# Centring the RWKV-7 values before the scan, and evicting each gram by one masked product

## The chip, the cores and the metric

The kernel runs on one NeuronCore of a Trainium2 chip. The metric is the device time of one execution in microseconds (us); what is compared is the median of the runs. A difference of 0.3% is about 9 us here.

The core has a matrix engine (PE, with its weight loads shown apart as PEld), a vector engine (DVE), an activation engine (ACT), a general engine (POOL) and a queue that issues most transfers (SP). Each engine works through its own instructions in the order in which they were put there.

## The reference

A decoder trunk of two layers over 1024 tokens of width 1024. Layer 0 mixes tokens with an RG-LRU, layer 1 with RWKV-7; each layer then has cross-attention into 256 memory tokens and a squared-ReLU MLP, and every part is wrapped in RMS norms. The change touches only the RWKV-7 mixer. Per head (16 heads of 64), a 64x64 state runs over the tokens, and the 64 outputs of a token are normalised to mean zero and unit variance:

```python
def step(state, inp):
    r_t, w_t, k_t, v_t, a_t, b_t = inp
    sa = einsum('bhij,bhj->bhi', state, a_t)
    state = state * w_t + sa[..., None] * b_t + v_t[..., None] * k_t
    y_t = einsum('bhij,bhj->bhi', state, r_t)
    return state, y_t
mean = jnp.mean(y, axis=-1, keepdims=True)
var = jnp.mean(jnp.square(y - mean), axis=-1, keepdims=True)
yn = (y - mean) * lax.rsqrt(var + RWKV_GN_EPS)      # then gain gn_g, offset gn_b
bonus = jnp.sum(rh * kh * r_k, axis=-1, keepdims=True) * vh
out = (yn + bonus) * g @ w_o
```

The index i of the state comes from the value v alone, and everything that is done to the state is linear in v. So subtracting from each v its mean over i subtracts from each y its mean over i. The bonus uses v itself.

## The kernel before, in words

All matrix work is in float32, in two ways: large products as three products of split halves (`mm3`, L317 to L319), small ones as one float32 product (`mm`). The trace records such a float32 product as two MATMUL records, a transpose as one.

The mixer `rwkv` goes through K, R and V phases, each a loop over eight blocks f of 128 features, and then the scan. In the V phase `evac_v(f)` copies the finished block `vt` (features x tokens) from PSUM (L1488), turns it to tokens by eight transposes of 128x128 in two PSUM banks (L1503), copies each bank to `vk` on ACT (L1504), stores `vk` to DRAM in `Vd` and forms the bonus from the same `vt` (L1520, L1521).

The scan works through 16 chunks of 64 tokens, two chunks to a load of 128 tokens. The work of chunk c has three parts, interleaved in the text of the loop (L1699 to L1765):

- The recurrence: products W (L1723), a copy of W on ACT (L1725), products U (L1745), a scaling on DVE into `sv` (L1747), products S (L1753) and an addition on DVE into the next chunk's `sv` (L1755), which the next W needs. POOL forms the decayed state `pcs` from it (L1732). The output Y is accumulated by L1728 and L1761 and copied to `y` by ACT (L1763).
- The grams of chunk c+1 (`scan_gram`, groups 0 to 3): four products per group (L1618) into one bank; DVE multiplies the wanted parts by triangular masks into `gt` (twice L1621 on 64 partitions, once L1624); ACT copies two quarters of `mv` into the places of `gt` that no gram fills (twice L1623); PE transposes the keys that POOL scaled (`scan_scale`, L1606, then L1632), and ACT copies them into `gt` (L1633). A group's `gt` feeds W, S and Y of the next chunk.
- The norm of chunk c-1: `post_mean` sums y on DVE (L1643) and POOL turns the sum to minus the mean (L1644); `post_var` adds that on DVE (L1650), squares on ACT (L1651), sums on DVE (L1652), and POOL forms the reciprocal root (L1653, L1654); `post_norm` multiplies on DVE (L1660). `flip_out(c-2)` transposes back to features (L1667) and applies gain and bonus (L1672 on DVE, L1673 on POOL).

The order of instructions on each engine is not that of the text. A planner that knows costs and dependences places each instruction when its inputs are due, earlier text first; `behind` and `pin` bind an instruction behind those already traced on its engine. The square of L1651 is pinned: it comes behind the last ACT instruction of group 1 of the next gram.

Loads for a pair of chunks are issued one pair ahead on SP (`load`, L1561 and L1565; `load_solved`, L1576; `load_late`, L1589 and L1593). Behind the scan follows the output projection with `b_w_o`, whose weights are split on ACT and DVE (L232, L233) from chunk 13 on, while the scan still runs.

Of the kernel before, what the change touches and what calls it, by code (L numbers as in the profile page):

```python
# [7 lines left out]
F32 = mybir.dt.float32  # L8
F32R = mybir.dt.float32r
AF = mybir.ActivationFunctionType  # L10
ALU = mybir.AluOpType
AX = mybir.AxisListType
# [1084 lines left out]
def rwkv_consts(self):  # L1097
    nc = self.nc
    c = self.const
    self.omu = c([128, 48], "omu")  # L1100
    nc.vector.tensor_scalar(self.omu, self.colv("mu", 48), -1.0, 1.0, ALU.mult, ALU.add)
    self.w0h = c([128, 8], "w0h")
    nc.vector.tensor_scalar(self.w0h, self.colv("w0"), 0.5, None, ALU.mult)
    self.a0h = c([128, 8], "a0h")
    nc.vector.tensor_scalar(self.a0h, self.colv("a0"), 0.5, None, ALU.mult)
    self.kah = c([128, 8], "kah")
    nc.vector.tensor_scalar(self.kah, self.colv("k_a"), 0.5, None, ALU.mult)
    self.kam = c([128, 8], "kam")
    nc.vector.tensor_scalar(self.kam, self.colv("k_a"), -1.0, 1.0, ALU.mult, ALU.add)
    self.nkk = c([128, 8], "nkk")  # L1110
    nc.vector.tensor_scalar(self.nkk, self.colv("k_k"), -1.0, None, ALU.mult)

    self.ind = c([128, 2], "ind")
    nc.gpsimd.memset(self.ind, 0.0)
    nc.gpsimd.memset(self.ind[0:64, 0:1], 1.0)
    nc.gpsimd.memset(self.ind[64:128, 1:2], 1.0)

    self.id64 = c([128, 64], "id64")
    nc.vector.tensor_add(self.id64, self.ident[:, 0:64], self.ident[:, 64:128])

    self.mask1 = c([128, 128], "mask1")
    nc.gpsimd.memset(self.mask1, 1.0)
    self.mask2 = c([128, 64], "mask2")
    nc.gpsimd.memset(self.mask2, 1.0)
    for h in range(2):
        r = slice(h * 64, h * 64 + 64)

        nc.gpsimd.affine_select(self.mask1[r, 0:64], self.mask1[r, 0:64], pattern=[[1, 64]], base=0,
                                channel_multiplier=-1, compare_op=ALU.is_ge, fill=0.0)
        nc.gpsimd.affine_select(self.mask2[r, :], self.mask2[r, :], pattern=[[1, 64]], base=-1,  # L1130
                                channel_multiplier=-1, compare_op=ALU.is_ge, fill=0.0)
    self.db = c([128, 256], "db")
    self.pc = c([128, 128], "pc")

    self.ones = c([128, 128], "ones")
    nc.gpsimd.memset(self.ones, 0.0)
    for h in range(2):
        nc.gpsimd.memset(self.ones[h * 64:h * 64 + 64, h * 64:h * 64 + 64], 1.0)


def rwkv_make_mix(self, X, i, hf, out, js=range(KT // 2)):
# [58 lines left out]
def rwkv(self, X, xt, lw_wa, lw_g, post):  # L1200
    nc, I = self.nc, self.I
    mm = nc.tensor.matmul
# [19 lines left out]
    for hf in range(2):  # L1222
        o = hf * 512
# [12 lines left out]
        if hf:  # L1236
            h = maps[0][2]
# [4 lines left out]
    h = maps[1][2]  # L1242
# [10 lines left out]
    hr = [slice(0, 64), slice(64, 128)]  # L1253
# [231 lines left out]
    def evac_v(f, p):  # L1485
        cs = slice(f * 128, f * 128 + 128)
        vt = self.unit()
        nc.scalar.copy(vt, p)  # L1488
        if f == 1:

            self.depth, self.ahead = DA
            with self.behind():
                self.advance(self.taken - 1)
        pr, kp = ld.pop(f)
        nc.vector.scalar_tensor_tensor(pr, pr, self.col("r_k", f), kp, ALU.mult, ALU.mult)

        if f % 2 == 0:
            vk[:] = [self.unit() for _ in range(2)]
        for e in range(2):
            pt = self.bank()  # L1500
            for i in range(4):
                tt = e * 4 + i
                nc.tensor.transpose(pt[:, i * 128:i * 128 + 128], vt[:, tt * 128:tt * 128 + 128], self.ident)  # L1503
            nc.scalar.copy(vk[e].rearrange("p (t h g i) -> p t h g i", h=2, g=2, i=64)[:, :, :, f % 2, :],  # L1504
                           pt.rearrange("p (t h i) -> p t h i", h=2, i=64))
            if f % 2 and e == 0:

                for d in range(2):
                    for h in range(2):
                        nc.sync.dma_start(sv0[d][hr[1 - h], h * 512 + (f - 1) * 64:h * 512 + (f + 1) * 64],  # L1510
                                          vk[0].rearrange("p (t h i) -> p t h i", h=2, i=128)[hr[d], 0, h, :])
            if f % 2:
                for h in range(2):
                    nc.sync.dma_start(Vd[e * 512:e * 512 + 512, h, (f - 1) * 64:(f + 1) * 64].rearrange("(t p) i -> p t i", p=128),
                                      vk[e].rearrange("p (t h i) -> p t h i", h=2, i=128)[:, :, h, :])
        g1 = self.unit()
        for e in range(2):
            s = slice(e * 512, e * 512 + 512)
            bp = self.bank()
            mm(bp, self.ones, pr[:, s], start=True, stop=True)  # L1520
            nc.vector.tensor_mul(vt[:, s], vt[:, s], bp)  # L1521
            gp = self.bank()
            self.mm3(gp, (g2[0][:, cs], g2[1][:, cs]), (hg[0][:, s], hg[1][:, s]), True, True)
            nc.scalar.activation(g1[:, s], gp, AF.Copy, scale=self.col("gn_g", f))
            nc.vector.scalar_tensor_tensor(vt[:, s], vt[:, s], self.col("gn_b", f), gp, ALU.add, ALU.mult)
        for src, dst in ((g1, G1d), (vt, G2d)):
            for h in range(2):
                nc.sync.dma_start(dst[(f % 2) * 64:(f % 2) * 64 + 64, (f // 2) * 2 + h, :], src[h * 64:h * 64 + 64, :])
# [11 lines left out]
    cst, prs, z, mvb = {}, {}, [], []  # L1540
# [67 lines left out]
    def scan_gram(c, groups):  # L1608
        if c >= 16:
            return  # L1610
        s = cst[c]
        for g in groups:
            gt = self.unit()[:, 0:768].rearrange("p (q h w) -> p q h w", q=2, h=2)
            pv = self.bank(g).rearrange("p (q h w) -> p q h w", q=2, h=2)
            for pp in range(2):
                q = 2 * g + pp
                for h in range(2):
                    mm(pv[:, pp, h, :], s["st"][q // 4][:, q % 4].rearrange("p w t -> p (w t)"), s["mv"][:, q, h], start=True, stop=True)  # L1618
            for h in range(2):
                o = hr[1 - h]  # L1620
                nc.vector.tensor_tensor(gt[o, :, h, 0:64], pv[o, :, h, 0:64],  # L1621
                                        self.mask2[o].unsqueeze(1).broadcast_to([64, 2, 64]), ALU.mult)
                nc.scalar.copy(gt[hr[h], :, h, 0:64], s["mv"][hr[h], 2 * g:2 * g + 2, h, 0, :])  # L1623
            nc.vector.tensor_tensor(gt[:, :, :, 64:128], pv[:, :, :, 64:128],  # L1624
                                    self.mask1[:, 0:64].unsqueeze(1).unsqueeze(1).broadcast_to([128, 2, 2, 64]), ALU.mult)
            if c < 15:
                if g % 2 == 0:
                    s["tp"] = self.bank(g // 2).rearrange("p (q h i) -> p q h i", q=4, h=2)
                tp = s["tp"][:, 2 * (g % 2):2 * (g % 2) + 2]
                for pp in range(2):  # L1630
                    q = 2 * g + pp
                    nc.tensor.transpose(tp[:, pp].rearrange("p h i -> p (h i)"), s["sc"][:, q * 128:q * 128 + 128], self.ident)  # L1632
                nc.scalar.copy(gt[:, :, :, 128:192], tp)  # L1633
            s["gts"].append(gt)
# [2 lines left out]
    yq = lambda t: t.rearrange("p (q i) -> p q i", i=64)  # L1637
    over = lambda t: t.unsqueeze(2).broadcast_to([128, 8, 64])

    def post_mean(c):  # L1640
        s = cst[c]
        s["n"] = mean, var = [self.sp.tile([128, 8], F32, name=self.nm("g8"), tag="g8", bufs=8) for _ in range(2)]
        nc.vector.tensor_reduce(mean, yq(s["y"][:, 0:512]), op=ALU.add, axis=AX.X)  # L1643
        nc.gpsimd.tensor_scalar(mean, mean, -1.0 / 64, 0.0, ALU.mult, ALU.add)  # L1644

    def post_var(c):
        s = cst[c]
        y = s["y"]
        mean, var = s["n"]
        nc.vector.tensor_tensor(yq(y[:, 0:512]), yq(y[:, 0:512]), over(mean), ALU.add)  # L1650
        self.pin(nc.scalar.activation(y[:, 512:1024], y[:, 0:512], AF.Square))  # L1651
        nc.vector.tensor_reduce(var, yq(y[:, 512:1024]), op=ALU.add, axis=AX.X)  # L1652
        nc.gpsimd.tensor_scalar(var, var, 1.0 / 64, 64e-5, ALU.mult, ALU.add)  # L1653
        nc.gpsimd.tensor_tensor(var, var, self.nhalf[:, :8], ALU.pow)  # L1654

    def post_norm(c):
        s = cst[c]
        y = s["y"]
        mean, var = s["n"]
        POST(nc).tensor_tensor(yq(y[:, 0:512]), yq(y[:, 0:512]), over(var), ALU.mult)  # L1660

    def flip_out(c):
# [36 lines left out]
    for c in range(16):  # L1699
# [62 lines left out]
                   stop=(m == 1 and q == 3))  # L1762
        nc.scalar.copy(y[:, 0:512], yp)  # L1763
        s["y"] = y
        post_mean(c)  # L1765
    post_var(15)
    post_norm(15)
    self.depth, self.ahead = 2, 3
# [58 lines left out]
```

## Time and profile before

| what | value |
|---|---|
| median of 3 runs | 2956.07 us (2955.89, 2956.07, 2964.06) |
| the profiled execution, its own time | 2958.01 us |
| its span, first to last instruction | 2956.3 us |
| PE busy | 2846.8 us, 96% |
| DVE busy | 1807.8 us, 61% |
| ACT busy | 1365.6 us, 46% |
| POOL busy | 860.7 us, 29% |
| mean granted clock of PE | 0.988 of 2.4 GHz |

The busy shares are averages over stages that differ. The V phase lies between 1653 and 1780 us of the span, the scan between 1780 and 1984 us. A group of the trace gives a line of the code, the engine, the operation with its output and input, the shapes, the count, the busy time and the mean duration of one. The duration of a MATMUL record holds the way through the array, so records overlap; the time that a matmul costs is read from the distance between starts.

### The profile page before, as it was taken

To read this page: it belongs to the slowest core of one execution; us is meant where nothing else is said; L and a number is where in the kernel's file an instruction comes from. 1 tells how busy PE (TensorE), PEld (TensorE's weight loads), DVE (VectorE), ACT (ScalarE), POOL (GpSimd) and SP (SyncE) were. 2 spreads that over 40 slices of the span, in tenths; PEclk is the share of its full clock that TensorE was granted. 3 is DMA by queue.
4 is the path that set the end of the run, shared out by engine and by line. 5 is a ranking of instruction groups with operands and counts; after the bars stand their busy time and mean duration, and the time that the engine had idled before them with its cause. 6 is when DMAs were issued, how large, how long until landed. Compare 5 with 4: busy or idle time off the path is not lost.

```text
span 2956.3 us, 42688 instructions
## 1 busy us (share of the span) xinstructions
PE 2846.8 (96%) x16987; PEld 2373.4 (80%) x16987; DVE 1807.8 (61%) x2110; ACT 1365.6 (46%) x1981; POOL 860.7 (29%) x951
## 2 busy tenths in 40 slices
PE   7999999999999999999999998989999999999998
PEld 6888798887888888887777677878788788888886
DVE  5576552557455677877585626883345745557778
ACT  5465342446444543448552524452344544454333
POOL 2000110022666500021486215652002366650001
PEclk9999999999999999999999999999999999999999
DMA  7212362123444644432656989952312344464443
GB/s 255 78 49 74 98 207 75 48 83 98 157 149 149 239 166 152 164 114 94 182 158 191 236 217 220 205 137 93 100 43 79 100 146 157 153 224 175 157 170 115
DMA packets 383847, 421.91 MB, mean 143 GB/s; under 512 B 91440, under 2 KB 294432, under 8 KB 383648
## 3 DMA queue, kind: packets, MB, share of 16 engines
q1 hardware_dynamic: 371616, 379.19, 42.6%
q0 software_dynamic: 11568, 39.41, 3.7%
q8 instruction: 133, 2.18, 0.3%
q14 instruction: 66, 0.54, 0.1%
q10 hardware_dynamic: 464, 0.59, 0.1%
HBM read 283.79 MB, written 134.74 MB: 142 GB/s over the span
## 4 chain that ended last, share of the span: by engine, by line
PE 83%; DVE 7%; DMA 3%; issue 2%; ACT 2%; POOL 2%; SPq 1%; DVEq 0%; POOLq 0%; ACTq 0%
PE q L317 15%; PE q L319 15%; PE q L318 15%; PE p L317 11%; PE p L319 11%; PE p L318 11%; DVE u L233 2%; DMA u<-d 1%; PE q L1618 1%; DVE u L1158 1%; POOL u L1732 1%; ACT u L232 1%; PE q L358 0%; PE q L908 0%; PE q L383 0%
## 5 line engine op out<-in xcount | busy, mean ns | idle before, releaser
L233 DVE TENSOR_TENSOR u<-u,u 128x1024 fp32r<-128x1024 f32 (+1 forms) x550 | 741.5, 1379 | 354.0 <-ACT u L232 331.9
L232 ACT CAST u<-u 128x1024 fp32r<-128x1024 f32 (+1 forms) x550 | 541.8, 1022 | 407.4 <-DVE u L1002 224.9
L317 PE MATMUL q<-u,u 128*128 128x512 f32 (+2 forms) x1824 | 698.6, 385 | 9.8 <-ACT u L232 7.5
L318 PE MATMUL q<-u,u 128*128 128x512 f32 (+2 forms) x1824 | 697.9, 383 | 1.1 <-POOL u L365 0.5
L319 PE MATMUL q<-u,u 128*128 128x512 f32 (+2 forms) x1824 | 692.4, 383 | 0.5 <-DVE u L233 0.5
L317 PE MATMUL p<-u,u 128*128 128x512 f32 (+1 forms) x1728 | 657.6, 383 | 22.4 <-ACT u L232 9.8
L318 PE MATMUL p<-u,u 128*128 128x512 f32 (+1 forms) x1728 | 655.5, 379 | 5.9 <-DVE u L233 5.8
L319 PE MATMUL p<-u,u 128*128 128x512 f32 (+1 forms) x1728 | 653.6, 378 | 3.7 <-DVE u L233 3.7
L328 POOL TENSOR_SCALAR s<-s 128x1 f32<-128x1 f32 x98 | 39.3, 401 | 1446.5 <-ACT u L326 1427.1
L317 PEld LDWEIGHTS q<-u,u 128*128 128x128 f32 (+1 forms) x1824 | 343.7, 189 | 81.3 <-ACT u L232 8.9
L317 PEld LDWEIGHTS p<-u,u 128*128 128x128 f32 x1728 | 329.9, 191 | 87.8 <-ACT u L232 15.9
L318 PEld LDWEIGHTS q<-u,u 128*128 128x128 f32 (+1 forms) x1824 | 344.0, 189 | 68.7 <-DVE u L233 2.8
L319 PEld LDWEIGHTS q<-u,u 128*128 128x128 f32 (+1 forms) x1824 | 343.9, 189 | 67.3 <-DVE u L233 0.7
L318 PEld LDWEIGHTS p<-u,u 128*128 128x128 f32 x1728 | 330.8, 191 | 67.5 <-DVE u L233 9.6
L319 PEld LDWEIGHTS p<-u,u 128*128 128x128 f32 x1728 | 330.4, 191 | 64.8 <-DVE u L233 5.2
L1060 DVE TENSOR_TENSOR z<-z,q 128x512 f32<-128x512 f32 x192 | 130.3, 682 | 81.3 <-PE q L319 81.3
L430 POOL TENSOR_TENSOR u<-u,u 128x512 f32<-128x512 f32 x96 | 150.2, 1567 | 8.3 <-DMA u<-in_m_w_down 2.6
L319 PE MATMUL q<-z,u 128*128 128x512 f32 x256 | 99.8, 390 | 1.2 <-DVE u L233 1.2
L318 PE MATMUL q<-z,u 128*128 128x512 f32 x256 | 99.6, 389 | 0.0
L317 PE MATMUL q<-z,u 128*128 128x512 f32 x256 | 99.3, 389 | 0.0
L639 DVE SCALAR_TENSOR_TENSOR u<-p,s,u 128x1024 f32<-128x1024 f32 x24 | 30.8, 1284 | 109.1 <-ACT u L232 69.6
L957 POOL TENSOR_TENSOR u<-u,u 128x512 f32<-128x512 f32 x32 | 44.2, 1382 | 175.7 <-ACT u L946 158.5
(258 smaller groups left out, 3390.3 us busy)
## 6 DMA issues: line engine op xcount, KB each, us to landing
u<-d SPq DMA_DIRECT2D x198, 512.0 KB, 4.5
d<-u SPq DMA_DIRECT2D x109, 512.0 KB, 3.4
d<-u POOLq DMA_DIRECT2D x68, 512.0 KB, 3.2
d<-u SPq DMA_DIRECT2D x132, 256.0 KB, 3.6
u<-in_m_w_up SPq DMA_DIRECT2D x64, 512.0 KB, 5.5
u<-in_m_w_down SPq DMA_DIRECT2D x64, 512.0 KB, 8.3
u<-in_c_w_kv SPq DMA_DIRECT2D x32, 512.0 KB, 6.7
u<-d SPq DMA_DIRECT2D x56, 256.0 KB, 7.7
```

The source lines that it names most:

```text
L232: self.nc.scalar.copy(hv, src)
L233: (eng or self.nc.vector).tensor_tensor(lv, src, hv, ALU.subtract)
L317: mm(o, ah, bh, start=first, stop=False, **kw)
L318: mm(o, ah, bl, start=False, stop=False, **kw)
L319: mm(o, al, bh, start=False, stop=last, **kw)
L328: nc.gpsimd.tensor_scalar(v, ss, 1.0 / n, eps, ALU.mult, ALU.add)
L430: sub = lambda o, x, y: nc.gpsimd.tensor_tensor(o, x, y, ALU.subtract)
L639: nc.vector.scalar_tensor_tensor(o, src, r, gb, ALU.mult, ALU.mult)
L957: tt(s1, r21, r22, ALU.add)
L1060: nc.vector.tensor_add(to_, to_, o)
L1158: nc.vector.scalar_tensor_tensor(m[:, o + 1:o + 512], X[hf][:, k, :511], mu, m[:, o + 1:o + 512], ALU.mult, ALU.add)
L1618: mm(pv[:, pp, h, :], s["st"][q // 4][:, q % 4].rearrange("p w t -> p (w t)"), s["mv"][:, q, h], start=True, stop=True)
```

## The change

`rwkv_consts`: one mask of 128x128 (strict triangle in the left half, triangle with diagonal in the right half) takes the place of two, and a matrix `center` is added: the identity minus 1/64 inside each 64x64 diagonal block.

`evac_v`: the eight transposes become eight float32 products with `center` as the moving operand, which turn to tokens and subtract each head's mean in one step. The bonus still reads `vt`, uncentred.

`scan_gram`: one product over the whole bank (128x512) with the mask, in place of three. It also writes the two quarters that the ACT copies fill, so these copies now come behind it.

`post_mean` and the addition of the mean go; the square becomes eight squares of 64 columns, each with its sum taken by the ACT accumulator, all pinned; the sum on DVE goes.

```diff
+    self.center = c([128, 128], "center")
+    nc.vector.scalar_tensor_tensor(self.center, self.ones, -1.0 / 64, self.ident, ALU.mult, ALU.add)
...
-                nc.tensor.transpose(pt[:, i * 128:i * 128 + 128], vt[:, tt * 128:tt * 128 + 128], self.ident)
+                mm(pt[:, i * 128:i * 128 + 128], vt[:, tt * 128:tt * 128 + 128], self.center, start=True, stop=True)
...
+            gw = gt.rearrange("p q h w -> p (q h) w")
+            nc.vector.tensor_tensor(gw[:, :, 0:128], pv.rearrange("p q h w -> p (q h) w"),
+                                    self.mask.unsqueeze(1).broadcast_to([128, 4, 128]), ALU.mult)
+
             for h in range(2):
-                o = hr[1 - h]
-                nc.vector.tensor_tensor(gt[o, :, h, 0:64], pv[o, :, h, 0:64],
-                                        self.mask2[o].unsqueeze(1).broadcast_to([64, 2, 64]), ALU.mult)
                 nc.scalar.copy(gt[hr[h], :, h, 0:64], s["mv"][hr[h], 2 * g:2 * g + 2, h, 0, :])
-            nc.vector.tensor_tensor(gt[:, :, :, 64:128], pv[:, :, :, 64:128],
-                                    self.mask1[:, 0:64].unsqueeze(1).unsqueeze(1).broadcast_to([128, 2, 2, 64]), ALU.mult)
...
-        nc.vector.tensor_reduce(mean, yq(s["y"][:, 0:512]), op=ALU.add, axis=AX.X)
-        nc.gpsimd.tensor_scalar(mean, mean, -1.0 / 64, 0.0, ALU.mult, ALU.add)
...
-        nc.vector.tensor_tensor(yq(y[:, 0:512]), yq(y[:, 0:512]), over(mean), ALU.add)
-        self.pin(nc.scalar.activation(y[:, 512:1024], y[:, 0:512], AF.Square))
-        nc.vector.tensor_reduce(var, yq(y[:, 512:1024]), op=ALU.add, axis=AX.X)
+        for q in range(8):
+            self.pin(nc.scalar.activation(y[:, 512 + q * 64:576 + q * 64], y[:, q * 64:q * 64 + 64], AF.Square,
+                                          accum_out=var[:, q:q + 1]))
```

## Rows read from the trace of the kernel before

**Rows 1.** Windows: stretch, its length, busy time of each engine, clock, DMA share.

```profile
1653.40:1779.50 126.10, 115.59 (x1072) 88.25 (x1073) 38.07 (x49) 45.26 (x67) 28.01 (x43) 0.96 0.87 220
1813.00:1859.00 46.00, 43.46 (x772) 39.11 (x769) 39.53 (x94) 21.06 (x61) 31.50 (x39) 1.00 1.07 216
1859.00:1955.68 96.68, 91.42 (x1634) 82.76 (x1632) 83.58 (x199) 45.75 (x130) 66.42 (x80) 1.00 0.87 187
1955.68:1990.00 34.32, 28.22 (x423) 24.02 (x422) 31.96 (x61) 19.86 (x34) 15.53 (x16) 0.90 0.46 125
```

**Rows 2.** Waits of PE in the scan, 1779.5 to 1990 us: total, times, longest.

```profile
PE q L1632 <- POOL u L1606: 7.3, 6, 1.3
PE q L1761 <- DVE u L1747: 2.8, 4, 1.8
PE q L1723 <- DVE u L1755: 2.3, 3, 1.5
```

**Rows 3.** Chain of waits in order of time, 1911 to 1919 us: start, length, what.

```profile
1911.84 0.42 DVE u L1755
...
1912.98 0.61 DVE g L1643
...
1913.67 0.20 POOL g L1644
...
1913.95 1.12 POOL u L1732
...
1918.29 0.44 PE q L1632 x2
```

**Rows 4.** Timeline of PE, V phase: start, length, line, idle before in brackets.

```profile
1725.46 1.04 PE L1503 MATMUL q<-ident,u 128*128 128x128 f32 x8
1726.34 1.02 PE L1520 MATMUL q<-u,ones 128*128 128x512 f32 x2
```

**Rows 5.** Timeline of PE, one chunk of the scan, columns as in Rows 4.

```profile
1913.42 2.05 PE L1618 MATMUL q<-z,u 128*128 128x128 f32 x16
1915.31 0.60 PE L1667 MATMUL q<-ident,u 128*128 128x128 f32 x4
1915.84 1.15 PE L1745 MATMUL q<-u,u 64*64 64x64 f32 x32
```

**Rows 6.** Groups by line and shape, 1640 to 2060 us: busy, mean ns, idle before.

```profile
L1618 PE MATMUL q<-z,u 128*128 128x128 f32 x512 | 70.8, 286 | 6.0 <-DMA u<-d 5.7 <-DVE u L1624 0.2
L1623 ACT COPY u<-z 64x128 f32<-64x128 f32 x128 | 37.8, 295 | 1.9
L1621 DVE TENSOR_TENSOR u<-q,mask 64x128 f32<-64x128 f32 x128 | 36.9, 288 | 9.8 <-PE q L1618 7.0 <-POOL u L1606 0.4
L1624 DVE TENSOR_TENSOR u<-q,mask 128x256 f32<-128x256 f32 x64 | 26.0, 406 | 0.0
L1650 DVE TENSOR_TENSOR u<-u,g 128x512 f32<-128x512 f32 x16 | 11.2, 702 | 15.0 <-POOL g L1644 14.9
L1643 DVE TENSOR_REDUCE g<-u 128x8 f32<-128x512 f32 x16 | 10.9, 682 | 3.2 <-ACT u L1763 3.1
L1672 DVE TENSOR_TENSOR u<-q,u 128x512 f32<-128x512 f32 x16 | 10.8, 676 | 0.1
L1651 ACT ACTIVATE u<-u 128x512 f32<-128x512 f32 x16 | 10.1, 631 | 6.8 <-DVE u L1650 6.5
```

**Rows 7.** Timeline of ACT in the first layer's attention: activations with accumulator, columns as in Rows 4.

```profile
548.87 0.47 ACT L896 ACTIVATE u<-p,s 128x256 f32<-128x256 f32 x1
549.24 0.19 ACT L896 ACTIVATION_READ_ACCUMULATOR u<-p,s 128x1 f32 x1
549.33 0.47 ACT L896 ACTIVATE u<-p,s 128x256 f32<-128x256 f32 x1
```

**Rows 8.** Timeline of ACT, one chunk of the scan, columns as in Rows 4.

```profile
1920.87 0.37 ACT L1633 COPY u<-q 128x256 f32<-128x256 f32 x1 [1.09 <-PE q L1632]
...
1924.75 0.38 ACT L1725 COPY u<-q 128x256 f32<-128x256 f32 x1
```

More of the change, by code (lines that the diff above doesn't have):

```diff
@@ L1119, in rwkv_consts @@
     nc.vector.tensor_add(self.id64, self.ident[:, 0:64], self.ident[:, 64:128])
[L1121 to L1124, printed above, removed]
+    self.mask = c([128, 128], "mask")
+    nc.gpsimd.memset(self.mask, 1.0)
     for h in range(2):
         r = slice(h * 64, h * 64 + 64)
[L1128 to L1131, printed above, removed]
+        for i in range(2):
+            m = self.mask[r, i * 64:i * 64 + 64]
+            nc.gpsimd.affine_select(m, m, pattern=[[1, 64]], base=i - 1,
+                                    channel_multiplier=-1, compare_op=ALU.is_ge, fill=0.0)
     self.db = c([128, 256], "db")
@@ L1638, in rwkv @@
     over = lambda t: t.unsqueeze(2).broadcast_to([128, 8, 64])
-    def post_mean(c):
-        s = cst[c]
-        s["n"] = mean, var = [self.sp.tile([128, 8], F32, name=self.nm("g8"), tag="g8", bufs=8) for _ in range(2)]
-        nc.vector.tensor_reduce(mean, yq(s["y"][:, 0:512]), op=ALU.add, axis=AX.X)
-        nc.gpsimd.tensor_scalar(mean, mean, -1.0 / 64, 0.0, ALU.mult, ALU.add)
     def post_var(c):
@@ L1648, in post_var @@
         y = s["y"]
-        mean, var = s["n"]
-        nc.vector.tensor_tensor(yq(y[:, 0:512]), yq(y[:, 0:512]), over(mean), ALU.add)
-        self.pin(nc.scalar.activation(y[:, 512:1024], y[:, 0:512], AF.Square))
-        nc.vector.tensor_reduce(var, yq(y[:, 512:1024]), op=ALU.add, axis=AX.X)
+        var = s["n"] = self.sp.tile([128, 8], F32, name=self.nm("g8"), tag="g8", bufs=8)
+        for q in range(8):
+            self.pin(nc.scalar.activation(y[:, 512 + q * 64:576 + q * 64], y[:, q * 64:q * 64 + 64], AF.Square,
+                                          accum_out=var[:, q:q + 1]))
         nc.gpsimd.tensor_scalar(var, var, 1.0 / 64, 64e-5, ALU.mult, ALU.add)
@@ L1657, in post_norm @@
         s = cst[c]
-        y = s["y"]
-        mean, var = s["n"]
+        y, var = s["y"], s["n"]
         POST(nc).tensor_tensor(yq(y[:, 0:512]), yq(y[:, 0:512]), over(var), ALU.mult)
@@ L1764, in rwkv @@
         s["y"] = y
-        post_mean(c)
     post_var(15)
```

## The prediction

> **What bounds the kernel now.** I read the stretches first, then PE's waits in them, then the chain there, then the durations of what is added and removed.
>
> By stretches [rows 1], PE is busy 115.59 of 126.10 us in the V phase and 91.42 of 96.68 us in the even part of the scan: PE sets the pace in both. DVE, with 83.58 of 96.68 us, is close behind it in the scan; ACT has half of its time free (45.75). At the scan's end it is DVE (31.96 of 34.32 us) that is full, and PE idles 6.1 us at a mean clock of 0.90.
>
> PE's waits [rows 2] tell what its idle time in the scan is. Six times, for 7.3 us in all, a transpose L1632 waits for the scaled keys of POOL; 5.1 us are waits for DVE, the longest of 1.5 and 1.8 us in the last chunks. The chain [rows 3] says why POOL is late: L1644, the mean, stands ahead of L1732 on POOL and waits for the sum L1643 on DVE; four L1732 follow (the first of 1.12 us stands for them), then L1606, then PE's transpose at 1918.29, 1.3 us after PE was free. The reader should see that the norm is off the recurrence, and reaches it only through POOL's order. This recurs once per pair of chunks, 24.17 us (96.68 is four pairs).
>
> **The V phase, more work on PE.** Eight transposes in a row occupy PE from 1725.46 to 1726.34, 0.11 us each, with PE dense on both sides [rows 4]. A float32 product of the same shape is two records (512 for the 256 products of L1618 [rows 6]), and 16 records go from 1913.42 to 1915.31 [rows 5]: 0.236 us a product. So +0.126 us for each of 64 products: +8.1 us, on the path, as PE is full there. Below, 8% of the phase is PE idle [rows 1], and if as much of the addition fell into it, +7.4; above, see the third rival. The ACT copies behind them and `center` in the constants cost nothing that PE waits for: ACT is free for 81 of the 126 us. But the scan's first loads come behind the last stored block, so the start of the scan moves with it.
>
> The Trainium skill ("TensorE: Matmul & The Clock Gate", Terms) calls the transpose mode four times faster for float32. By it each product would add three transposes, 64 x 3 x 0.11 = +21 us. The two records of L1618 speak for a factor of two, and I take that.
>
> **The scan, work off DVE.** Per chunk four groups lose 2 x 0.288 + 0.406 us each and gain one 128x512 product out of PSUM, priced by L1672 at 0.676 [rows 6]: 0.306 x 4 = -1.2 us. The norm loses L1643, L1650 and L1652, 0.682 + 0.702 + 0.68 (a sum of L1643's shape) = -2.1 us. That is 3.3 us of about 10.4 busy per chunk. Off the path most of it costs nothing today, since PE has other work while DVE is behind.
>
> What it does move: with L1644 gone, L1732 starts when L1755 is done, about 1.7 us earlier (L1755 ends at 1912.26, L1732 starts at 1913.95 [rows 3]), so L1606 ends before PE asks. PE's 7.3 us go. Next late would be PE itself. For the shorter waits of W and U on DVE inside the pairs I add -1.5 us (ends 0 and, if DVE is the hidden bound, the second rival). In the last chunks DVE is the bound; two chunks lose 6.6 us of DVE work; I take -3.0, near the two longest waits (ends 0 and -6.1, all of PE's idle time in that stretch).
>
> **The scan, work onto ACT.** The square was 0.631 us for 512 columns, a copy of 128 columns is 0.295: 0.875 ns a column, so 0.239 us for 64. Activation and accumulator read together show 0.45 us between starts where the activation alone shows 0.47 and the read 0.19 [rows 7]: the pair overlaps by 0.21. So 0.239 + 0.19 - 0.21 = 0.22 us a square with its sum, and 8 x 0.22 = 1.8 in place of 0.6. Ends: 0.15 without the read, 0.43 with no overlap. ACT goes from 5.7 to 6.9 us busy of 12.1. But it is pinned behind group 1's L1633, and the queue from there to the next chunk's W copy L1725 (1921.24 to 1924.75 [rows 8], 3.5 us) then holds the squares 1.8, the copies of groups 2 and 3, which can no longer be drawn ahead as they now wait for the masked product (4 x 0.295 + 2 x 0.37 = 1.9), and L1763 (0.6): 4.3 us. It starts 1.3 us earlier with POOL's wait gone, so it fits: 0 on the path. The masked product before the ACT copies lengthens a group by 0.6 us; groups are made most of a chunk ahead, so again 0. Queued behind the squares are the copies of groups 2 and 3, L1763 and L1725, and W and U of the next chunk wait for these.
>
> **Sum.** +8.1 - 7.3 - 1.5 - 3.0 = -3.7 us against this execution's 2958.0, which is 1.9 above the median: 2954.3 in its own time, 2952.4 as a median. About 0.3%, 9 us, is what can be told from no change here.
>
> **The rivals.**
>
> First, slower: ACT's queue becomes the loop's bound. If the pair of square and read does not overlap (0.43 us), the queue above holds 3.4 + 1.9 + 0.6 = 5.9 us against 3.5 + 1.3: 1.1 us late in each of 14 chunks, +15, and nothing of the 7.3 is kept. 8.1 + 15 - 3 = +20: 2976. It decides from 0.29 us a square on. For it: everything in the queue is in order and the recurrence is last in it. Against: rows 7. The Trainium skill speaks for this side ("VectorE: DVE Perf Modes", the TRN2 errata): small ScalarE operations out of SBUF pay a fixed latency each, best amortised over 512 elements or more; the 0.239 above, of which 0.18 does not scale with columns, agrees, and the overlap is what it leaves out. Chance 0.12.
>
> Second, faster: the scan was paced by DVE's latencies all along, and PE falls to what its records need: 32 of L1618 at 0.118, 12 transposes at 0.12, 160 small records at 0.033 (L1745, x32 in about 1.05 us [rows 5]): 10.5 us a chunk rather than 12.1. Over 12 chunks -19, with the end's -3 and the +8.1: -14, and with the waits at the start of each product group also gone up to -19. I price it at 2940. For it: DVE at 86% in order. Against: rows 2 show few waits for it. Chance 0.20.
>
> Third, a product costs four transposes: +21 for +8.1, the sum +9.2: 2965. Chance 0.03.
>
> Fourth, no gain in the scan: loads bound it. Their share is 1.07 of the DMA engines up to 1859 us and 0.87 after [rows 1]; a shorter pair asks for the same loads in less time, and POOL's L1606 needs them. Then the 7.3 and the 1.5 stay, 8.1 - 3 = +5: 2961. For it: the share. Against: the chain of a pair after 1859 us [rows 3] passes through no load. Chance 0.13.
>
> That the change does not do what it says is no rival: centring is linear, and each removed instruction is gone from the text.
>
> **How the numbers follow.** My forecast has 0.52, at 2952, its own range 2944 to 2960. The whole range, 2938 to 2966, leaves out the first rival, and the far ends of the second. Faster by over 0.3% is below 2947: the second rival and 0.10 of the forecast, 0.30. Slower by over 0.3% is above 2965: the first, about half of the third and 0.05 of the fourth, 0.19. The rest is 0.51.
>
> **What would show it.** V phase: 128 records on the line of the new product and 8 us more between the first of them and the first L1618. Scan: no wait of L1632 for L1606, a pair in 22.5 to 23 us, DVE at 7.1 us busy a chunk, ACT near 6.9 and squares 0.22 apart; W's copies not behind squares. The end: PE idle under 4 us. I would be wrong in kind if PE waited for ACT in every chunk, or if the pair fell below 22 us; wrong in size if the new product's starts are not 0.24 us apart. The new order that the planner makes is not in any row, and could move the layers behind the scan by a few us.

## The result, and the profile after

The median fell from 2956.35 us (2955.89 to 2964.06, 4 runs) to 2937.29 us (2932.61 to 2941.34, 4 runs): a ratio of 0.9936, 95% interval 0.9923 to 0.9948, or 19.1 us less. The forecast was 2952 with a range from 2938, so the kernel became faster than foreseen, by 15 us. The profiled execution took 2941.34 us, the slowest of its four, with a span of 2939.6 us.

The page of after, row of the engines: engine, busy time with its share of the span, instructions.

```profile
PE 2846.5 (97%) x17051; PEld 2375.3 (81%) x17051; DVE 1763.7 (60%) x1935; ACT 1386.3 (47%) x2221; POOL 854.7 (29%) x934
```

PE does as much work as before; it waits less. Where, is seen by stages cut at the same instructions in both kernels: the V phase up to the first gram; the start (first gram to W of chunk 2); the even part (to W of chunk 14); the end (to the first product of the output projection). First after, then before; columns: stretch, length, busy PE, PEld, DVE, ACT, POOL, PEclk, DMA share, GB/s. These answer to [rows 1], with other cuts.

```profile
1650.10:1781.70 131.60, 122.05 (x1136) 96.21 (x1137) 38.29 (x49) 45.83 (x65) 27.97 (x43) 0.97 0.86 216
1781.70:1810.43 28.73, 26.44 (x441) 24.07 (x440) 16.26 (x31) 15.87 (x58) 14.81 (x17) 1.00 1.03 247
1810.43:1948.08 137.65, 135.88 (x2455) 122.64 (x2453) 94.15 (x170) 83.12 (x373) 96.47 (x109) 1.00 1.00 211
1948.08:1965.21 17.13, 15.04 (x337) 13.79 (x333) 14.07 (x25) 13.18 (x52) 8.48 (x10) 1.00 0.68 176
```

```profile
1653.40:1779.70 126.30, 115.79 (x1072) 88.44 (x1073) 38.27 (x49) 45.37 (x67) 28.01 (x43) 0.96 0.87 220
1779.70:1814.14 34.44, 27.98 (x441) 25.66 (x440) 19.83 (x56) 13.94 (x42) 14.61 (x17) 0.90 0.97 233
1814.14:1960.53 146.39, 138.02 (x2448) 124.52 (x2448) 126.71 (x302) 68.65 (x194) 99.44 (x120) 1.00 0.92 193
1960.53:1983.63 23.10, 17.78 (x329) 15.50 (x329) 20.91 (x41) 12.92 (x25) 9.29 (x11) 0.96 0.57 155
```

The reader should see three things. The V phase is 5.3 us longer (126.3 before), and the start 5.7 us shorter, at a clock of 1.00 where it was 0.90. In the even part PE's idle time fell from 8.4 to 1.8 us, while DVE went from 87% to 68% of it. At the end DVE fell from 20.91 to 14.07 us, and the stretch by 6.0.

| us | before V | V | start | even part | end | behind | span |
|---|---|---|---|---|---|---|---|
| before | 1653.4 | 126.3 | 34.4 | 146.4 | 23.1 | 972.7 | 2956.3 |
| after | 1650.1 | 131.6 | 28.7 | 137.6 | 17.1 | 974.4 | 2939.6 |
| difference | -3.3 | +5.3 | -5.7 | -8.7 | -6.0 | +1.7 | -16.7 |

The other 2.4 us of the 19.1 lie between these two profiled executions and the medians of their kernels (4.1 above it after, 1.7 before). Apart from the constants, the code before V and behind the scan is the same; these -1.6 us stay unexplained.

PE's waits in the scan of after, 1780 to 1985 us (total, times, longest). They answer to [rows 2]: the wait for POOL's keys is gone, and no other of its size took its place.

```profile
PE q L1722 <- issue: 1.5, 1, 1.5
PE q L1717 <- issue: 1.3, 1, 1.3
PE q L1620 <- PE q L1722: 0.7, 1, 0.7
PE q L1755 <- DVE u L1741: 0.7, 2, 0.5
```

The same view of before has a second large line, which [rows 2] does not show: PE's wait for a load at the start of the scan. In after, the waits of 1.3 and 0.7 us above lie there.

```profile
PE q L1618 <- DMA u<-d: 5.7, 1, 5.7
```

The chain of waits of after, 1860 to 1950 us, summed by line. It answers to [rows 3], where a pair's chain went through DVE and POOL; now it is PE's own instructions, with 2% of issue.

```profile
by line: PE q L1620 33.0%; PE q L1755 12.2%; PE q L1633 11.8%; PE q L1739 11.6%; PE q L1722 9.1%; PE q L1747 8.6%; PE q L1717 8.3%; PE q L1661 3.5%; issue 2.0%
```

Groups of after by line and shape, 1640 to 2100 us (busy, mean ns, idle before), which answer to [rows 6]: the product with `center` is L1505, the masked product L1622, the copies of `mv` L1626, the squares L1646.

```profile
L1622 DVE TENSOR_TENSOR u<-q,mask 128x512 f32<-128x512 f32 x64 | 44.1, 691 | 34.9 <-PE q L1620 34.4 <-DMA u<-d 0.2
L1626 ACT COPY u<-z 64x128 f32<-64x128 f32 x128 | 37.9, 296 | 41.5 <-DVE u L1622 35.6 <-DMA u<-d 3.8 <-POOL u L1608 0.3
L1646 ACT ACTIVATE u<-u 128x64 f32<-128x64 f32 x128 | 30.8, 242 | 0.2
L1646 ACT ACTIVATION_READ_ACCUMULATOR u<-u 128x1 f32 x128 | 24.0, 187 | 0.0
L1505 PE MATMUL q<-center,u 128*128 128x128 f32 x128 | 18.4, 299 | 3.6 <-DVE u L1527 1.9 <-ACT u L1489 1.5
```

ACT in one chunk of after (start, length, line), which answers to [rows 8]: squares 0.24 to 0.26 us apart with their reads between, then the keys' copy, then the copy of W. The squares begin at 1873.71 and the last read starts at 1875.54.

```profile
1873.71 0.26 ACT L1646 ACTIVATE u<-u 128x64 f32<-128x64 f32 x1
1873.87 0.19 ACT L1646 ACTIVATION_READ_ACCUMULATOR u<-u 128x1 f32 x1
1873.97 0.24 ACT L1646 ACTIVATE u<-u 128x64 f32<-128x64 f32 x1
...
1875.54 0.19 ACT L1646 ACTIVATION_READ_ACCUMULATOR u<-u 128x1 f32 x1
1875.64 0.35 ACT L1634 COPY u<-q 128x256 f32<-128x256 f32 x1
...
1878.90 0.38 ACT L1719 COPY u<-q 128x256 f32<-128x256 f32 x1
```

### The profile page after: what moved, and what is told of

Same layout as the page of the kernel before. It is cut to its first block, busy times and chain, and to the rows that moved or that the text cites. A ratio compares the mean times of both kernels' runs of the same rounds, so it can differ in the third digit from the quotient of the medians.

```text
span 2939.6 us, 42857 instructions
## 1 busy us (share of the span) xinstructions
PE 2846.5 (97%) x17051; PEld 2375.3 (81%) x17051; DVE 1763.7 (60%) x1935; ACT 1386.3 (47%) x2221; POOL 854.7 (29%) x934
## 4 chain that ended last, share of the span: by engine, by line
PE 43%; DVE 3%; DMA 2%; SPq 1%; ACT 1%; issue 1%; DVEq 0%; POOLq 0%; POOL 0%; ACTq 0%
PE q L317 7%; PE q L319 7%; PE q L318 7%; PE p L317 5%; PE p L318 5%; PE p L319 5%; PE q L1620 2%; DVE u L233 1%; DMA u<-d 1%; DVE u L1159 1%; PE q L1633 1%; PE q L1755 1%; DMA u<-in_b_w_rkv 1%; PE q L1739 1%; PE q L1722 1%
## 5 line engine op out<-in xcount | busy, mean ns | idle before, releaser
L232 ACT CAST u<-u 128x1024 fp32r<-128x1024 f32 (+1 forms) x550 | 541.8, 1022 | 406.0 <-DVE u L1002 224.8
L318 PEld LDWEIGHTS p<-u,u 128*128 128x128 f32 x1728 | 330.8, 191 | 69.5 <-DVE u L233 11.3
L430 POOL TENSOR_TENSOR u<-u,u 128x512 f32<-128x512 f32 x96 | 151.2, 1578 | 8.3 <-DMA u<-in_m_w_down 2.6
L639 DVE SCALAR_TENSOR_TENSOR u<-p,s,u 128x1024 f32<-128x1024 f32 x24 | 30.8, 1284 | 110.4 <-ACT u L232 71.7
L326 ACT ACTIVATE u<-u 128x1024 f32<-128x1024 f32 x58 | 61.4, 1060 | 74.3 <-DVE u L780 50.9
```

Source lines behind the costliest of these rows:

```text
L232: self.nc.scalar.copy(hv, src)
L318: mm(o, ah, bl, start=False, stop=False, **kw)
L326: nc.scalar.activation(junk, src, AF.Square, accum_out=ss)
L430: sub = lambda o, x, y: nc.gpsimd.tensor_tensor(o, x, y, ALU.subtract)
L639: nc.vector.scalar_tensor_tensor(o, src, r, gb, ALU.mult, ALU.mult)
```

## The experiments

Two theories ran against each other. A is the prediction's: V's products stand on the path with their 8 us, and the pairs gain by POOL's order, L1644 ahead of L1732. B: V's products fill waits that PE has anyway, and the pairs were paced by DVE's queue, 87% full; PE's wait for POOL was only the form in which that showed. Each comparison is with runs of before on the same chip. Stages of all kernels, cut as above (us). A pair is two chunks; given is the median of the six pairs of the even part. In the profiled execution of after two of the six took 23.1 and 24.2 us, so its even part is longer than six times 22.6:

| kernel | V | start | even part | end | pair |
|---|---|---|---|---|---|
| before | 126.3 | 34.4 | 146.4 | 23.1 | 24.2 |
| after | 131.6 | 28.7 | 137.6 | 17.1 | 22.6 |
| identity product | 130.3 | 32.3 | 146.4 | 22.4 | 24.2 |
| product twice | 136.8 | 31.0 | 146.3 | 22.9 | 24.1 |
| after, transposes | 124.2 | 33.0 | 135.4 | 17.1 | 22.6 |
| mean on DVE | 124.2 | 33.6 | 146.5 | 21.9 | 24.2 |
| mask only | 122.6 | 33.0 | 140.9 | 21.0 | 23.4 |
| centre only | 128.0 | 31.7 | 136.6 | 20.9 | 22.3 |
| centre, padded | 127.5 | 31.8 | 144.2 | 23.0 | 23.8 |
| after, POOL waits | 121.8 | 28.3 | 136.9 | 17.6 | 22.8 |
| after, sum on DVE | 129.5 | 29.2 | 135.8 | 21.0 | 22.6 |
| after, old masks | 133.7 | 30.8 | 134.6 | 20.7 | 22.3 |
| after, early splits | 132.2 | 29.0 | 137.8 | 17.1 | 22.6 |

V's length differs by up to 12 us between kernels whose V phase is the same (the reason stands under the hardware below), so it is read together with the start and with the medians.

### The V phase alone

Before, with its 64 transposes as products with the identity:

```diff
-                nc.tensor.transpose(pt[...], vt[...], self.ident)
+                mm(pt[...], vt[...], self.ident, start=True, stop=True)
```

> The kernel before, with the eight transposes of each V block turned into eight float32 products with the identity, and nothing else: the price of the V phase by itself. Theory A (the prediction's term): +8 us, on the path. Theory B: the 5.7 us for which PE waits at the start of the scan for the second pair's loads do not hang on PE's pace in the V phase, so most of the added work is taken out of that wait: the V phase is 5 to 8 us longer, the stretch from the first gram to the third chunk 4 to 6 us shorter, 0 to +3 us in all.

2957.70 us (11 runs) against 2957.34; ratio 0.9999 (0.9990 to 1.0008), so between -3.0 and +2.4 us. The work is there: from start to start the product line takes 18.0 us in all where the transposes took 10.8. The time is not. PE's longest wait at the start of the scan in this kernel, for a load:

```profile
PE q L1618 <- DMA u<-d: 2.7, 1, 2.7
```

In before the same wait is 5.7 us. The awaited load did come later, but by less than PE. SP issued it 141.6 us behind the first transpose of V in before and 143.4 us behind it here, while V is 4.0 us longer. The issues are (start, length, line; before, identity product, product twice):

```profile
1794.95 8.08 SPq L1561 DMA_DIRECT2D u<-d  x4
```

```profile
1796.91 8.15 SPq L1561 DMA_DIRECT2D u<-d  x4
```

```profile
1800.38 7.68 SPq L1562 DMA_DIRECT2D u<-d  x4
```

Within V, PE's idle time fell from 10.5 to 8.2 us. So B's total came, but not its split: V is 4.0 us longer and the start 2.1 shorter, where 5 to 8 and 4 to 6 were expected, and A's +8 lies outside the interval. The same from the other end: after, with transposes in place of the products with `center` (the mean over each head is left out).

> The changed kernel with the eight transposes of each V block in the place of the eight products, so that no mean is subtracted at all: the scan as changed, the V phase as before. Theory A (each product is paid for): 7 to 8 us faster than the changed kernel. Theory B (the added work falls into waits for loads, in the V phase and at the scan's start): 0 to 3 us faster, the V phase 4 us shorter and the stretch from the first gram to the third chunk 2 to 4 us longer.

2937.21 us against 2955.29 for before; ratio 0.9936 (0.9924 to 0.9948), the same ratio as after. PE's wait at the start of the scan, and then the V phase and the start, in this kernel:

```profile
PE q L1620 <- issue: 4.8, 1, 4.8
```

```profile
1653.00:1777.20 124.20, 115.89 (x1073) 88.25 (x1073) 38.30 (x49) 44.77 (x65) 27.92 (x42) 0.97 0.91 225
1777.20:1810.20 33.00, 27.92 (x439) 25.76 (x439) 16.17 (x31) 15.77 (x58) 14.79 (x17) 0.90 0.95 230
```

V is 7.4 us shorter than in after, the start 4.3 longer: PE is back to waiting, and the clock of the stretch is back at 0.90. (B had expected 4 us, and 2 to 4.) If the gaps are only so wide, more work must begin to cost. Before with each identity product made twice:

```diff
+                for _ in range(2):
+                    mm(pt[...], vt[...], self.ident, start=True, stop=True)
```

> The kernel before with each of the 64 transposes turned into the same product with the identity, issued twice: 64 x 0.236 = 15.1 us of PE more than with one product each, 22 more than with transposes. Theory A (the work is on the path, and the first product cost nothing only by the spread of the runs): +14 to +16 us against the run with one product, +14 to +22 against the kernel before. Theory B (waits for loads of some 6 us take it in, then it is paid for): +8 to +12 us against the kernel before, and PE's wait for loads at the start of the scan gone.

2966.66 us against 2955.29; ratio 1.0041 (1.0029 to 1.0053), 12 us more. Its V phase:

```profile
1651.40:1788.20 136.80, 133.18 (x1265) 107.87 (x1266) 38.84 (x49) 46.11 (x67) 27.90 (x43) 1.00 0.79 206
```

PE is busy for 133.18 us there where before, in the same cut, had 115.79; of these 17.4 us about 5 were free by the medians (2 to 9 by the interval). In this profile PE's idle time in V fell from 10.5 to 3.6 us, as the longest wait there is gone (it is shown under the hardware below), and the wait at the start of the scan fell from 5.7 to 2.4 us. It is not gone, as B had expected: SP issued the load 149.0 us behind the first product of V, 7.4 us later than in before. (The profiled execution is the fastest of its six, 2962.91, so its stages add up to less than the 12.)

### The pairs: POOL's order or DVE's queue

First, before with L1644, the mean's scaling, on DVE, so that POOL's queue has nothing ahead of L1732 that waits for the sum:

```diff
-        nc.gpsimd.tensor_scalar(mean, mean, -1.0 / 64, 0.0, ALU.mult, ALU.add)
+        nc.vector.tensor_scalar(mean, mean, -1.0 / 64, 0.0, ALU.mult, ALU.add)
```

> The kernel before, with the one POOL instruction that scales the mean (128x8) put on DVE: it takes 1 us off nothing, adds about 0.2 us a chunk to DVE, and takes the wait for the sum out of POOL's queue. Theory A (POOL's order is what the pairs wait for): the waits of L1632 for L1606 go, a pair falls from 24.17 to about 22.8 us, -6 to -9 us in all. Theory B (DVE's load is what paces the pairs): no change or up to +3 us, as DVE gets more to do.

2953.50 us against 2957.34; ratio 0.9991 (0.9982 to 0.9999). PE's waits from 1810 to 1955 us, and the moved instruction's group:

```profile
PE q L1723 <- DVE u L1755: 2.9, 5, 0.6
...
PE q L1632 <- POOL u L1606: 0.3, 1, 0.3
```

```profile
L1644 DVE TENSOR_SCALAR g<-g 128x8 f32<-128x8 f32 x16 | 10.5, 656 | 0.3
```

The wait for POOL's keys is gone (7.3 us before), and the pair is 24.2 us as before: PE waits for DVE instead. Against A, but not clean, as the instruction loaded DVE with 0.66 us a chunk, not with the 0.2 that were expected. The clean one is after, with the old chain put back to no use: the sum of y on DVE, and its scaling on POOL where L1644 stood.

```diff
         s["y"] = y
+        nc.vector.tensor_reduce(mean, yq(y[:, 0:512]), op=ALU.add, axis=AX.X)
+        nc.gpsimd.tensor_scalar(mean, mean, -1.0 / 64, 0.0, ALU.mult, ALU.add)
```

> The changed kernel with the sum on DVE and its scaling on POOL put back as they stood, and thrown away: POOL's queue waits for the sum again, DVE stays 2.6 us a chunk lighter than before. Theory A (POOL's order paces the pairs): pairs at 23.5 to 24.2 us, +7 to +9 us against the changed kernel. Theory B (DVE's queue paces them): pairs within 0.4 us of the changed kernel's 22.6, 0 to +4 us.

2937.50 us against 2955.35; ratio 0.9943 (0.9930 to 0.9957). POOL's wait for the sum from 1812 to 1950 us of this kernel, then from 1812 to 1955 us of before, then PE's wait for POOL in this kernel:

```profile
POOL g L1761 <- DVE g L1760: 10.3, 5, 2.1
```

```profile
POOL g L1644 <- DVE g L1643: 13.2, 6, 3.1
```

```profile
PE q L1633 <- POOL u L1608: 0.7, 4, 0.2
```

POOL waits for the sum for up to 2.1 us, ahead of the decay in its queue, a little shorter than in before. PE's transposes then wait 0.7 us in all; the pair is 22.8 us, and the gain stays. So with DVE light POOL's order costs 0.2 us a pair, and A's mechanism does not explain the gain. Then B's: before with the masked product alone, POOL's queue untouched.

```diff
-                nc.vector.tensor_tensor(gt[o, :, h, 0:64], ..., ALU.mult)           # twice
-            nc.vector.tensor_tensor(gt[:, :, :, 64:128], ..., ALU.mult)
+            nc.vector.tensor_tensor(gw[:, :, 0:128], pv..., self.mask..., ALU.mult)
```

> The kernel before, with one mask of 128x128 and one masked product per gram, the mean and the squares as before: DVE 1.2 us a chunk lighter, the ACT copies behind the product, POOL's queue untouched. Theory A (POOL's order paces the pairs): pairs stay at 24 us, the end gains 1 us, 0 to -3 us in all. Theory B (DVE's load paces them): 1 us off each chunk, -10 us or more. Theory C (the copies behind the product cost something): slower by 2 to 7 us.

2945.86 us against 2957.34; ratio 0.9963 (0.9950 to 0.9975), -11 us, for 1.2 us less on DVE a chunk. The pair fell by 0.8 us, to 23.4, where B had 1 us for each chunk. The wait for POOL (here L1629 for L1604) is still there but shorter; its 0.7 us a pair is about what this pair has above 22.6:

```profile
PE q L1629 <- POOL u L1604: 4.3, 6, 0.7
```

The other half: after with the old masks, and the norm's squares as one instruction of 512 columns with a sum on DVE; so of the norm only the sum of y, the mean's scaling on POOL and its addition go.

```diff
-        for q in range(8):
-            self.pin(nc.scalar.activation(y[...], y[...], AF.Square, accum_out=var[...]))
+        self.pin(nc.scalar.activation(y[:, 512:1024], y[:, 0:512], AF.Square))
+        nc.vector.tensor_reduce(var, yq(y[:, 512:1024]), op=ALU.add, axis=AX.X)
```

> The change with the masks of before, and with one square of 512 columns on ACT and the sum on DVE as before: centring by the product alone. DVE 1.4 us a chunk lighter, ACT as before. Theory A (POOL's order): pairs at 22.6 to 23 us, -10 to -15 us in all, the larger part of the change. Theory B (DVE's load): half of what the change gains in the pairs, 23.4 us a pair, -6 to -9 us in all.

2944.29 us; ratio 0.9954 (0.9942 to 0.9967). The pair is 22.3 us, already PE's own. By itself that is what A expected, and more than B did. What tells the theories apart is the same kernel with DVE's load put back, and nothing for POOL to wait for: a sum of y thrown away and a zero added to y, on DVE.

```diff
         s["y"] = y
+        nc.vector.tensor_reduce(self.pad, yq(y[:, 0:512]), op=ALU.add, axis=AX.X)
...
+        nc.vector.tensor_tensor(yq(y[:, 0:512]), yq(y[:, 0:512]), over(self.zero8), ALU.add)
```

> Centring by the product alone, as in the run before it, with the two DVE instructions that it saved put back where they stood: the sum is formed and thrown away, and a zero is added in the place of the mean. DVE carries what it did before, and only POOL's scaling of the mean is gone. Theory A (POOL's order paces the pairs): pairs stay at 22.3 us, no change against the run without the padding. Theory B (DVE's queue paces them, POOL's wait was one form of it): pairs back at 23.5 to 24.2 us, +8 to +12 us against the run without the padding, the time of the kernel before within 4 us.

2952.01 us against 2955.35; ratio 0.9983 (0.9974 to 0.9992): 8.6 of the 13.6 us that the half was worth are lost again by the added instructions. PE's waits from 1812 to 1950 us, and four pairs of this kernel, DVE busy 87.60 of 95 us:

```profile
PE q L1723 <- DVE u L1755: 2.9, 5, 0.6
```

```profile
1860.00:1955.00 95.00, 91.78 (x1611) 82.11 (x1607) 87.60 (x199) 45.59 (x129) 65.62 (x72) 1.00 0.81 182
```

A pair of 23.8 us with DVE at 92%; 22.6 with DVE at 68%. B holds in the main: the load without the wait brings back most of the pair's length, the wait without the load 0.2 us. Not all comes back: this kernel is still 5.0 us (2.4 to 7.7) faster than before, 2.2 of it in the even part of its profile, so POOL's order may count for something while DVE is full. The waits of PE that show DVE's part are at most 0.6 us each.

### The end

After with the norm's sum on DVE (the square as one instruction, as in the diff above), and after with the old masks:

> The change with one square of 512 columns on ACT and the sum on DVE, as before: ACT 1.2 us a chunk lighter, DVE 0.7 us heavier. Theory A and B alike, as PE paces the pairs in both: within 3 us of the changed kernel; if ACT's eight squares hold the recurrence's copies anywhere, 2 to 6 us faster than it. If DVE's queue still paces parts, 2 to 5 us slower.

> The change with the masks of before: DVE 1.2 us a chunk heavier, the ACT copies free of the product again. With PE pacing the pairs: within 3 us of the changed kernel. If the end of the scan is paced by DVE: 2 to 4 us slower than the changed kernel, all of it in the last two chunks.

2939.46 us, ratio 0.9955 (0.9942 to 0.9967), and 2943.09 us, 0.9965 (0.9953 to 0.9978). By the medians that is 2.2 and 5.8 us above after; for the old masks 2 to 4 had been expected, all of it at the end. In both the pairs keep their gain (22.6 and 22.3), and the end does not: 21.0 and 20.7 us against 17.1. The scaling of U in the last chunk on DVE (start, length, line): first with the sum on DVE, then in after.

```profile
1963.62 0.86 DVE L1740 TENSOR_TENSOR u<-q,db 64x256 f32<-64x256 f32 x2
1964.52 1.23 DVE L233 TENSOR_TENSOR u<-u,u 128x1024 fp32r<-128x1024 f32 x1
1965.77 0.88 DVE L1740 TENSOR_TENSOR u<-q,db 64x256 f32<-64x256 f32 x2
```

```profile
1962.03 1.77 DVE L1741 TENSOR_TENSOR u<-q,db 64x256 f32<-64x256 f32 x4
1963.83 2.36 DVE L233 TENSOR_TENSOR u<-u,u 128x1024 fp32r<-128x1024 f32 x2
```

A weight split for the output projection stands between the two halves of U's scaling, and the products behind it wait (1.7 us in two waits, beside 0.5 in after); the same order stands with the old masks. That this order is the cause is not shown: with the mask alone the four scalings are together, and its end is 21.0 us too. Putting those splits one pair earlier in after (`max(0, n - 3)` for `max(0, n - 4)`) shortened nothing:

> The changed kernel with the splits of the output weights begun one pair of chunks earlier, now that DVE is free for a third of each chunk: a version to beat both. If DVE's splits are what stands between the last chunks' steps: the stretch from chunk 14 to the first product of the output 1 to 3 us shorter, 0 to -3 us in all. Rival: the splits hold buffers that the scan's loads need, and pairs get longer: +2 to +6 us.

2939.34 us, ratio 0.9941 (0.9927 to 0.9956); the end is 17.1 as in after.

## Why the prediction was wrong, point by point

**The V phase, +8.1 us on the path: this step failed.** The price of the work was right: 18.9 us from start to start on the product's line against 10.8, a factor of 1.7. The Trainium skill's factor of four for transposes ("TensorE: Matmul & The Clock Gate", Terms), from which the prediction estimated +21, is not what the trace shows, and the third rival is out. Wrong was "on the path, as PE is full there". PE idled for 10.5 us in V and waited 5.7 us more for a load at the start of the scan, in a line that [rows 2] leaves out and [rows 6] has behind L1618. The lower end of +7.4 let idle time take in only 8% of the addition, without a reason. The runs showed that the idle time took in all of one product's extra work, 0.4 us (-3.0 to +2.4) for 7.2 us of it, and that 17.4 us cost 12. That the start of the scan moves with the last stored block was right in direction: the awaited load was issued 1.6 us later in after, 1.8 with the identity product and 7.4 with the doubled one, behind a V longer by 5.3, 4.0 and 10.5 us. This step is 8.5 of the 13 us by which the sum missed the two profiles: V and start together came to -0.4, to which the lighter work at the start of the scan contributes.

**The pairs, -7.3 and -1.5: near in size, wrong in mechanism.** -8.8 was said, -8.7 measured in this profile (-11.0 in that of after with transposes, whose scan is the same), and the pair of 22.6 us lay in the 22.5 to 23 foreseen. But that the norm reaches the recurrence only through POOL's order does not hold: the wait can stay at POOL (after, POOL waits) or go from it (mean on DVE) with little change in the pairs. What counted in the main was the lighter DVE, of whose relief "off the path most of it costs nothing today" was said. Its busy time fell by 2.7 us a chunk, from 10.6 to 7.8, where 3.3 and 7.1 were foreseen. That is the mechanism of the second rival, "the scan was paced by DVE's latencies", which had 0.20. Its floor of 10.5 us a chunk was not reached (11.3), and its total of 2940 came close by luck, because V's 8.1, which it kept too, was not paid. The waits for POOL in [rows 2], which seemed to speak against it, were in the main DVE's lateness passed on: POOL itself waited there for DVE's sum.

**The end, -3.0: half of the measured 6.0.** The reason agrees with the rows, DVE being full there (20.91 of 23.1 us), and the far end of its bound was named at -6.1. The two edits are not additive here: either alone leaves about 21 us, both give 17.1, and why is open.

**ACT, 0: right.** The pair of square and read takes 0.26 and less from start to start (0.22 said, 0.29 the point from which it would decide), ACT is busy 6.9 us a chunk as foreseen, and PE waits for no ACT instruction in the pairs. The copies L1626 wait 35.6 us in all for the masked product, and PE waits for none of them in the pairs. The Trainium skill's errata on small ScalarE operations ("VectorE: DVE Perf Modes", the TRN2 errata), which stood behind the first rival, name a fixed latency for each. The trace agrees: 242 ns for 64 columns beside 631 ns for 512 [rows 6] leave some 0.19 us that do not scale with columns; the queue had the room for it.

**The masked product** was priced at 0.676 us and takes 0.691. The loads, fourth rival, did not bind: their share rose from 0.92 to 1.00 in the even part, and no load stands in the chain from 1860 to 1950 us.

**Not settled.** The start's -5.7 us is in part the V products in the wait (-2.1 with the identity product) and in part the lighter grams (-1.4 with the mask alone); the rest was not separated. These are single profiles, and the waits in them differ by some microseconds. Whether the 1.8 us of idle time left in the even part could go was not tried.

## What to carry to other kernels

An engine that is busy for 92% of a stage can still take more work for nothing, if there are waits in the stage or behind it whose end moves less than the work: look at these waits, and at what ends them, before an addition is priced as on the path. When an engine waits for a second one that waits for a third, look which of them is nearly full: DVE at 87% was in the main the bound here, although the waits named another engine. To tell the two apart, put the wait back without the load, and the load without the wait.

## What the runs showed of the hardware

In the V phase PE has one long wait whose end its own row does not name ("issue"). It differs between profiles, also of kernels with the same work there: before, then after with POOL waiting, and after with the old masks.

```profile
PE q L1414 <- issue: 5.8, 1, 5.8
```

```profile
PE q L1415 <- issue: 0.7, 1, 0.7
```

```profile
PE q L1417 <- issue: 8.6, 1, 8.6
```

It accounts for most of the spread of V in the table, 7.9 of the 11.9 us between the last two. The rows of ACT and PE in before show what ends it (start, length, line):

```profile
1742.13 1.04 ACT L232 CAST u<-u 128x1024 fp32r<-128x1024 f32 x1 [13.30 <-DMA u<-in_b_w_rkv]
...
1744.70 1.18 ACT L1409 COPY u<-q 32x512 f32<-32x512 f32 x2
```

```profile
1745.38 0.28 PE L1414 MATMUL q<-u,u 32*32 32x32 f32 x2 [5.78 <-issue]
```

The products of L1414 read what the copies of L1409 write, and those stand on ACT behind the split L232, which waits for a block of weights. In twelve of the thirteen kernels PE goes on 0.67 to 0.68 us after the first of these copies starts; ACT's wait for the weights is 8.0 us with the wait of 0.7 and 15.9 with that of 8.6. In the thirteenth, product twice, PE comes later than the copies and does not wait. So the landing of the weights ends this wait, and V's products fill it as far as they bring PE there later.

A wait also costs behind its end. After the 4.8 us at the start of the scan with transposes, eight gram records take 2.04 us, where the same eight in after take 1.13, and the granted clock of the stretch behind the wait is 0.50, the lower of the two levels:

```profile
1799.80 2.04 PE L1620 MATMUL q<-z,u 128*128 128x128 f32 x8 [4.80 <-issue]
```

```profile
1799.80:1803.10 3.30, 3.30 (x15) 3.30 (x16) 0.69 (x1) 0.76 (x3) 2.04 (x2) 0.50 0.96 227
```

And a scaling of 128x8 numbers took DVE 656 ns on average, beside 288 for a masked 64x128 block [rows 6] and 0.20 us for the same instruction on POOL [rows 3]: a small shape was no small price.
